# Moving the weights of the first sub-block of each group to another place in a 256-byte line

## The chip, the cores and the metric

The kernel runs on one NeuronCore of a Trainium2 chip. The metric is the device time of one execution in microseconds (us); lower is better. The kernel before takes 1067.77 us, the median of three runs (1066.1, 1067.77 and 1069.37 us).

## The reference

One layer of a decoder trunk in float32. The input x is 256 tokens by 2048 channels; sixteen learned tokens are put in front of it, so that 272 tokens pass through. With h the stream of tokens:

```
u = rms_norm(h, g1)
u = u @ w_in + b_in                    # 2048 -> 4096, split into a and g
u = a * sigmoid(g)
u = causal depthwise convolution of width 31 + b_dw
u = silu(layer_norm(u))
u = u @ w_out + b_out                  # 2048 -> 2048
h = h + rms_norm(u, g2)
u = rms_norm(h, g3)
u = (silu(u @ w_gate) * (u @ w_up)) @ w_down     # 2048 -> 5632 -> 2048
h = h + rms_norm(u, g4)                # the sixteen tokens are dropped at the end
```

Nearly all the arithmetic is in the four products with weights: "in" (w_in), "out" (w_out), "gu" (gate and up together) and "down".

## The kernel before

**Weights.** All weights come from HBM as one flat stream that the host laid out in the order of use. It is cut into 360 sub-blocks of 128 partitions by 1024 float32 (fewer where a block of the contraction ends). `plan()` (line 42) lists them: for each of the four products, for each group of output tiles, for each run of `kb` contraction tiles. A sub-block holds `kb` contraction tiles times `n` output tiles of 128 by 128. `load` (line 138) issues its DMA from SyncE into a ring of four raw tiles. `prep` (line 149) splits it: ScalarE rounds it to fp32r into the tile `hi` (line 158), then VectorE, or GpSimd for some, writes the rest `raw - hi` into the tile `lo` (line 160). Both tiles have rings of four buffers.

**Places.** A `hi` or `lo` buffer has 1024 + 64 elements for each partition (4352 bytes, 17 lines of 256 bytes), and the weights may begin at any of its first 64 elements. `PLACES` (line 61) gives the two starts in elements: "out" and "gu" have `hi` at 16 and `lo` at 0, which is 64 and 0 bytes; "in" has 0 and 128 bytes; "down" has 0 and 0. The activations that stream against them lie in the tile `moving`, whose rows are 2304 bytes long, nine lines of 256.

**Products.** In "out" and "gu" the weights are the stationary operand. The activations are split into a high and a low part in the same way, 256 columns each, side by side. Each 128 by 128 tile of weights takes two matmuls (a pair below): `hi` against 512 columns, high and low parts together (line 230), and `lo` against the 256 columns of the high part (line 231). Every matmul has its own weight load, because the weights change each time. "in" takes three matmuls of 272 columns for each tile (lines 221 to 223). The last group of "out" takes three matmuls of 256 columns (line 226). In "down" the activations are stationary and the weights stream, 512 columns at a time (lines 778 to 780).

**Groups.** "out" has six groups, of 4, 4, 4, 2, 1 and 1 output tiles; "gu" has 22 groups, each of two gate tiles and two up tiles. Sixteen contraction tiles make a full sum. A group of "gu" is 64 pairs in eight sub-blocks of eight pairs. The full groups of "out" are the same; the groups with 2, 1 and 1 tiles have 4, 2 and 2 sub-blocks, each with eight weight tiles. The first group of "out" and the first group of "gu" run while their activations are still being made (layer norm, and residual with RMS norm), so their matmuls wait for them here and there.

**Order.** The order on TensorE, ScalarE, VectorE and GpSimd is that of the program text. `ahead` keeps up to three sub-blocks prepared in front of the one in use. Work that empties the accumulators of a group is put into `pending` and done in stages at the ends of the next sub-blocks. One such stage in the second group of "gu" is `factor` (line 684): it holds an fp32 matmul (line 686) with a sum of squares, between the pairs of that group.

Of the kernel before, what the change touches and what calls it, by code (L numbers as in the profile page):

```python
# [41 lines left out]
def plan():  # L42
    out = []
    for name, groups, n_k in (
        ("in", IN_GROUPS, NK),
        ("out", OUT_GROUPS, NK),
        ("gu", FFN_GROUPS, NK),
        ("down", DOWN_GROUPS, NF),
    ):
        for g, tiles in enumerate(groups):  # L50
            n = len(tiles) * (2 if name == "gu" else 1)
            for k, kb in sub_blocks(n, n_k):
                out.append((name, g, n, k, kb))
    return out


PLAN = plan()
FIRST = {name: [p[0] for p in PLAN].index(name) for name in ("in", "out", "gu", "down")}

LINE = 64  # L60
PLACES = {"in": (0, 32), "out": (16, 0), "gu": (16, 0), "down": (0, 0)}
MOVE = 2 * L + 32


def places(name, g):
    return PLACES[name]


# [19 lines left out]
def conformer_swiglu_kernel(ctx: ExitStack, tc: tile.TileContext, xT, wflat, vec, w_dw, gain, out):  # L88
# [17 lines left out]
    def moving(cols, nm):  # L106

        t = xs.tile([P, NK, MOVE], F32R, tag="moving", name=nm)
        return t[:, :, :cols]
# [28 lines left out]
    def load(i):  # L138
        if i >= len(PLAN) or i in raws:
            return  # L140
        _, _, n, _, kb = PLAN[i]
        sz = n * kb * P
        raw = wp.tile([P, SB], F32, tag="raw", name="raw", bufs=RAW)
        nc.sync.dma_start(
            out=raw[:, :sz], in_=wflat[offs[i] : offs[i] + P * sz].rearrange("(p f) -> p f", p=P)
        )
        raws[i] = raw

    def prep(i):
        name, g, n, _, kb = PLAN[i]  # L150
        sz = n * kb * P
        for j in range(i, i + RAW):
            load(j)
        raw = raws.pop(i)
        hi_at, lo_at = places(name, g)
        hi = wp.tile([P, SB + LINE], F32R, tag="hi", name="hi")[:, hi_at : hi_at + SB]
        lo = wp.tile([P, SB + LINE], F32R, tag="lo", name="lo")[:, lo_at : lo_at + SB]
        nc.scalar.copy(out=hi[:, :sz], in_=raw[:, :sz])  # L158
        eng = nc.gpsimd if i < FIRST["out"] + 10 or 0 <= i - FIRST["gu"] < 10 else nc.vector
        eng.tensor_tensor(  # L160
            out=lo[:, :sz], in0=raw[:, :sz], in1=hi[:, :sz].bitcast(F32), op=ALU.subtract
        )
        ready[i] = (hi, lo)

    def ahead(i, n):

        while n and state["next"] <= min(i + LOOK, len(PLAN) - 1) and state["next"] < state["cap"]:
            prep(state["next"])
            state["next"] += 1
            n -= 1  # L170
# [571 lines left out]

    free = xs.tile([P, NK * MOVE], F32, tag="moving", name="free")
    tr = free[:, : NK * SEQ].rearrange("p (c t) -> p c t", c=NK)
# [178 lines left out]
```

## Time and profile before

| | |
|---|---|
| median of 3 runs | 1067.77 us |
| the profiled execution's own time | 1068.15 us |
| its span, first to last instruction | 1066.4 us |
| TensorE matmuls busy | 1052.4 us, 99% of the span |
| TensorE weight loads busy | 935.5 us, 88% |
| VectorE, ScalarE, GpSimd busy | 692.8, 584.1, 321.3 us |
| granted TensorE clock, mean | 0.998 |
| HBM read | 192.35 MB, 182 GB/s over the span |

A group of the profile is a source line on one engine, with the tiles that it writes and reads, the number of instructions, and their busy time. Matmuls are pipelined: the recorded length of one (0.28 us for 256 columns) overlaps the next. The number that tells the pace is the distance from one start to the next, which is the busy time of a gapless stretch divided by the number of pairs in it.

### The profile page before, as it was taken

Reading aid. Unit: us, or ns where it says so; the run is one execution under the profiler, and the core shown is the slowest. Engines: PE = TensorE matmul, PEld = TensorE weight load, DVE = VectorE, ACT = ScalarE, POOL = GpSimd, SP = SyncE. Lnnn points to the kernel's source line nnn. Section 1 sums busy time; section 2 is a strip of 40 time slices with the busy share of each in tenths; the row PEclk is TensorE's granted clock in tenths of the full one; section 3 lists DMA queues with packets and bytes.
Section 4 is the critical chain, followed back from the end, with each engine's and each line's share of the span. In section 5 each row is a group of like instructions: output and inputs, shape, how many; then the busy total and the mean of one; then the engine's idle time right before and its main releaser. Section 6 shows DMA issues by size and latency. Waiting matters only on the chain.

```text
span 1066.4 us, 16373 instructions
## 1 busy us (share of the span) xinstructions
PE 1052.4 (99%) x6142; PEld 935.5 (88%) x6142; DVE 692.8 (65%) x1193; ACT 584.1 (55%) x918; POOL 321.3 (30%) x191
## 2 busy tenths in 40 slices
PE   9999999999999999999999999999999999999996
PEld 8999999988898888888888888888888888888885
DVE  5699999987437966555665556655666635454544
ACT  6877877767567654444454445444444434343432
POOL 4889999955245112111111111111111000000000
PEclk9999999999999999999999999999999999999999
DMA  7555566526654666666666666666666797666662
GB/s 252 175 171 172 178 177 173 166 65 212 186 178 129 217 186 191 186 190 188 188 186 190 192 186 191 184 193 184 193 181 195 206 265 223 197 195 192 190 195 97
DMA packets 71840, 197.62 MB, mean 185 GB/s; under 512 B 22992, under 2 KB 24528, under 8 KB 71632
## 3 DMA queue, kind: packets, MB, share of 16 engines
q1 hardware_dynamic: 61728, 192.90, 60.7%
q10 hardware_dynamic: 10032, 3.67, 1.5%
q8 instruction: 48, 0.79, 0.3%
q14 instruction: 32, 0.26, 0.1%
HBM read 192.35 MB, written 2.10 MB: 182 GB/s over the span
## 4 chain that ended last, share of the span: by engine, by line
PE 96%; DVE 1%; DMA 1%; ACT 1%; issue 0%; SPq 0%; POOL 0%; DVEq 0%; ACTq 0%; POOLq 0%
PE bank L230 36%; PE bank L231 18%; PE bank L780 7%; PE bank L779 7%; PE bank L778 7%; PE bank L222 6%; PE bank L223 6%; PE bank L221 6%; DMA raw<-wflat 1%; PE bank L419 1%; PE bank L226 1%; ACT hi L158 0%; SPq L112 0%; POOL lo L160 0%; DVE free L835 0%
## 5 line engine op out<-in xcount | busy, mean ns | idle before, releaser
L158 ACT CAST hi<-raw 128x1024 fp32r<-128x1024 f32 x360 | 377.4, 1049 | 421.8 <-PE bank L230 189.3
L160 DVE TENSOR_TENSOR lo<-raw,hi 128x1024 fp32r<-128x1024 f32 x276 | 341.0, 1236 | 319.4 <-ACT hi L158 317.8
L230 PE MATMUL bank<-h_mv,hi 128*128 128x512 f32 x1408 | 492.2, 394 | 1.2 <-DVE h_mv L650 1.2
L231 PE MATMUL bank<-h_mv,lo 128*128 128x256 f32 x1408 | 395.1, 281 | 0.0
L230 PEld LDWEIGHTS bank<-h_mv,hi 128*128 128x128 f32 x1408 | 264.5, 188 | 60.6 <-issue 1.3
L231 PEld LDWEIGHTS bank<-h_mv,lo 128*128 128x128 f32 x1408 | 267.1, 190 | 0.0
L160 POOL TENSOR_TENSOR lo<-raw,hi 128x1024 fp32r<-128x1024 f32 x84 | 201.3, 2407 | 49.3 <-ACT hi L158 47.3
L720 POOL TENSOR_TENSOR hid<-sw_s,hid 128x256 fp32r<-128x256 f32 x44 | 64.8, 1474 | 416.2 <-ACT hid L719 416.2
L221 PE MATMUL bank<-x_mv,hi 128*128 128x272 f32 x512 | 147.6, 288 | 0.9 <-ACT x_mv L315 0.5
L222 PE MATMUL bank<-x_mv,hi 128*128 128x272 f32 x512 | 147.9, 289 | 0.4
L223 PE MATMUL bank<-x_mv,lo 128*128 128x272 f32 x512 | 147.7, 289 | 0.0
L778 PE MATMUL bank<-hi,hid 128*128 128x512 f32 x352 | 137.0, 389 | 0.0
L780 PE MATMUL bank<-hi,hid 128*128 128x512 f32 x352 | 136.9, 389 | 0.0
L779 PE MATMUL bank<-lo,hid 128*128 128x512 f32 x352 | 136.9, 389 | 0.0
L395 DVE SCALAR_TENSOR_TENSOR bank<-u,taps,bank 128x256 f32<-128x256 f32 x293 | 130.4, 489 | 1.7 <-ACT bank L388 1.7
L221 PEld LDWEIGHTS bank<-x_mv,hi 128*128 128x128 f32 x512 | 96.4, 188 | 2.1 <-ACT sig L354 1.0
L222 PEld LDWEIGHTS bank<-x_mv,hi 128*128 128x128 f32 x512 | 96.2, 188 | 1.1 <-DVE x_mv L316 1.1
L223 PEld LDWEIGHTS bank<-x_mv,lo 128*128 128x128 f32 x512 | 96.2, 188 | 0.0
L230 PE MATMUL bank<-s_mv,hi 128*128 128x512 f32 x240 | 84.8, 397 | 0.9 <-DVE s_mv L579 0.9
L778 PEld LDWEIGHTS bank<-hi,hid 128*128 128x128 f32 x352 | 66.1, 188 | 13.8
L779 PEld LDWEIGHTS bank<-lo,hid 128*128 128x128 f32 x352 | 66.1, 188 | 13.8
L780 PEld LDWEIGHTS bank<-hi,hid 128*128 128x128 f32 x352 | 66.1, 188 | 13.6
(139 smaller groups left out, 826.6 us busy)
## 6 DMA issues: line engine op xcount, KB each, us to landing
raw<-wflat SPq DMA_DIRECT2D x360, 512.0 KB, 3.6
x_sb<-xT SPq DMA_DIRECT2D x3, 544.0 KB, 4.9
x_sb<-free SPq DMA_DIRECT2D x16, 64.0 KB, 4.7
x_sb<-free ACTq DMA_DIRECT2D x16, 64.0 KB, 5.1
free<-gain ACTq DMA_DIRECT2D x1, 1024.0 KB, 8.5
y<-free ACTq DMA_DIRECT2D x8, 128.0 KB, 2.4
y<-free ACTq DMA_DIRECT2D x2, 256.0 KB, 2.4
y<-free SPq DMA_DIRECT2D x2, 256.0 KB, 2.8
```

Of the source, the lines that this page charges most:

```text
L158: nc.scalar.copy(out=hi[:, :sz], in_=raw[:, :sz])
L160: eng.tensor_tensor(out=lo[:, :sz], in0=raw[:, :sz], in1=hi[:, :sz].bitcast(F32), op=ALU.subtract)
L221: nc.tensor.matmul(banks[t][:, :L], lhsT=hi[:, s], rhs=xh[:, kk, :], start=kk == 0, stop=False)
L222: nc.tensor.matmul(banks[t][:, :L], lhsT=hi[:, s], rhs=xl[:, kk, :], start=False, stop=False)
L223: nc.tensor.matmul(banks[t][:, :L], lhsT=lo[:, s], rhs=xh[:, kk, :], start=False, stop=kk == n_k - 1)
L230: nc.tensor.matmul(banks[t], lhsT=hi[:, s], rhs=moving[:, kk, :], start=kk == 0, stop=False)
L231: nc.tensor.matmul(banks[t][:, :SEQ], lhsT=lo[:, s], rhs=moving[:, kk, :SEQ], start=False, stop=kk == n_k - 1)
L395: nc.vector.scalar_tensor_tensor(out=t if j == nd - 1 else o, in0=u[:, j : j + SEQ], scalar=taps[:, c, j : j + 1], in1=o, op0=ALU.mult, op ...
L720: nc.gpsimd.tensor_tensor(out=hl, in0=ts[2], in1=hh.bitcast(F32), op=ALU.subtract)
L778: nc.tensor.matmul(bs[h], lhsT=xh, rhs=hi[:, s], start=f == 0, stop=False)
L779: nc.tensor.matmul(bs[h], lhsT=xh, rhs=lo[:, s], start=False, stop=False)
L780: nc.tensor.matmul(bs[h], lhsT=xl, rhs=hi[:, s], start=False, stop=f == NF - 1)
```

## The change

The first sub-block of each group of "gu", and of each group of "out" but the first, has its `hi` part at element 0 and its `lo` part at element 48 (0 and 192 bytes of a line of 256). All other sub-blocks keep their places. No instruction is added, removed or reordered; the tiles keep their sizes. 27 of the 360 sub-blocks are touched: 22 in "gu" and 5 in "out".

```diff
 LINE = 64
 PLACES = {"in": (0, 32), "out": (16, 0), "gu": (16, 0), "down": (0, 0)}
+OTHER = (0, 48)
 MOVE = 2 * L + 32
 
-def places(name, g):
+def places(name, g, k0, kb):
+    if k0 == 0 and (name == "gu" or name == "out" and g):
+        return OTHER
     return PLACES[name]
...
     def prep(i):
-        name, g, n, _, kb = PLAN[i]
+        name, g, n, k0, kb = PLAN[i]
...
-        hi_at, lo_at = places(name, g)
+        hi_at, lo_at = places(name, g, k0, kb)
```

## Rows read from the trace of the kernel before

**Rows 1.** The page: span, busy time by engine, granted clock by slice, chain's engines

```profile
span 1066.4 us, 16373 instructions
...
PE 1052.4 (99%) x6142; PEld 935.5 (88%) x6142; DVE 692.8 (65%) x1193; ACT 584.1 (55%) x918; POOL 321.3 (30%) x191
...
PEclk9999999999999999999999999999999999999999
...
PE 96%; DVE 1%; DMA 1%; ACT 1%; issue 0%; SPq 0%; POOL 0%; DVEq 0%; ACTq 0%; POOLq 0%
```

**Rows 2.** Groups by line, TensorE, 400 to 800 us (gu): count, busy us, mean ns

```profile
L230 PE MATMUL bank<-h_mv,hi 128*128 128x512 f32 x1144 | 400.4, 394 | 0.0
L231 PE MATMUL bank<-h_mv,lo 128*128 128x256 f32 x1143 | 321.2, 281 | 0.0
```

**Rows 3.** The same, 335 to 360 us (gu, groups 0 and 1)

```profile
L230 PE MATMUL bank<-h_mv,hi 128*128 128x512 f32 x75 | 25.5, 389 | 0.0
L231 PE MATMUL bank<-h_mv,lo 128*128 128x256 f32 x74 | 20.4, 276 | 0.0
```

**Rows 4.** Timeline of TensorE, 361 to 363.3 us: start, length, line

```profile
360.64 0.39 PE L230 MATMUL bank<-h_mv,hi 128*128 128x512 f32 x1
...
360.98 0.39 PE L230 MATMUL bank<-h_mv,hi 128*128 128x512 f32 x1
361.21 0.28 PE L231 MATMUL bank<-h_mv,lo 128*128 128x256 f32 x1
361.42 0.67 PE L686 MATMUL bank<-acc,ones 128*128 128x256 f32 x2
361.74 0.58 PE L230 MATMUL bank<-h_mv,hi 128*128 128x512 f32 x1
...
362.27 0.40 PE L230 MATMUL bank<-h_mv,hi 128*128 128x512 f32 x1
...
362.97 0.40 PE L230 MATMUL bank<-h_mv,hi 128*128 128x512 f32 x1
```

**Rows 5.** Timeline of TensorE, 229 to 233 us (start of out)

```profile
229.20 0.50 PE L230 MATMUL bank<-s_mv,hi 128*128 128x512 f32 x1 [0.94 <-DVE s_mv L579]
229.54 0.28 PE L231 MATMUL bank<-s_mv,lo 128*128 128x256 f32 x1
```

**Rows 6.** Timeline of TensorE, 245 to 249.8 us (out, group 0)

```profile
245.30 0.40 PE L230 MATMUL bank<-s_mv,hi 128*128 128x512 f32 x1
...
246.72 0.47 PE L230 MATMUL bank<-s_mv,hi 128*128 128x512 f32 x1
```

**Rows 7.** Timeline of TensorE, 322 to 331.5 us (start of gu)

```profile
327.26 0.45 PE L230 MATMUL bank<-h_mv,hi 128*128 128x512 f32 x1
327.55 0.28 PE L231 MATMUL bank<-h_mv,lo 128*128 128x256 f32 x1
327.66 0.39 PE L230 MATMUL bank<-h_mv,hi 128*128 128x512 f32 x1
...
331.06 0.39 PE L230 MATMUL bank<-h_mv,hi 128*128 128x512 f32 x1
```

**Rows 8.** Groups by line, TensorE, 253 to 313 us (out, groups 1 to 4)

```profile
L230 PE MATMUL bank<-s_mv,hi 128*128 128x512 f32 x173 | 60.6, 395 | 0.0
```

**Rows 9.** Busy time by stretch: PE, PEld, DVE, ACT, POOL, clock, DMA share, GB/s

```profile
100.00:200.00 100.00, 100.00 (x798) 100.00 (x797) 97.11 (x259) 78.16 (x149) 96.16 (x52) 1.00 0.60 174
...
500.00:600.00 100.00, 100.00 (x573) 87.80 (x573) 61.31 (x82) 47.69 (x73) 11.79 (x8) 1.00 0.63 189
...
830.00:1030.00 200.00, 200.00 (x884) 165.62 (x883) 99.25 (x92) 82.17 (x88) 0.00 (x0) 1.00 0.74 210
```

**Rows 10.** Waits, 400 to 800 us: who for whom, total us, times, longest

```profile
DVE lo L160 <- ACT hi L158: 157.7, 127, 1.6
ACT hi L158 <- PE bank L230: 147.1, 90, 1.8
```

## The prediction

> **What bounds the kernel now.** I read the page first. [...] The change alters no count of matmuls or columns, only where in a line of 256 bytes some weights lie; what it can change is the distance from one matmul's start to the next.
>
> I therefore read that distance next, from gapless stretches: busy time over count. From 400 to 800 us, in "gu", a pair (one `hi` matmul of 512 columns, one `lo` matmul of 256) takes 400.4 / 1144 = 350.0 ns [rows 2]. From 335 to 360 us the same pair takes 25.5 / 75 = 340.0 ns [rows 3]. [...]
>
> The timeline shows where the one becomes the other. Up to 360.98 us `hi` matmuls start 340 ns apart; then the fp32 matmul of `factor` comes between, and from 362.27 us on they start 350 ns apart [rows 4]. Nothing brings the pace back: rows 2 still have 350.0 over 1144 pairs. "out" shows the same number, 60.6 / 173 = 350.3 ns [rows 8]. The pace is thus something into which the stream falls after a disturbance, and which it keeps. The timeline of the two starts of "out" and "gu", where matmuls wait for activations, says more: I count 16 restarts after such a wait (the first at 229.20 us [rows 5], the one before the last at 327.26 us [rows 7], the last that of rows 4). After 7 of them the pairs follow at 340 ns, after 8 at 350, after one at (246.72 - 245.30) / 4 = 355 [rows 6]. The restart of rows 7 shows the good case: from 327.66 to 331.06 us there are ten pairs, 340 each.
>
> What differs between the paces must be how the weight loads of the next matmul fall against the columns that stream for the present one; both are read from the same memory at the same time. That is my inference. The rows show three paces, not their cause.
>
> **The change, part by part.** *Instructions.* None is added or removed. ScalarE's and VectorE's writes of the 27 moved sub-blocks go to other bytes of the same buffers. I take that at nothing, and it is covered: in "gu" ScalarE stands waiting for TensorE to free a buffer for 147.1 us of 400 [rows 10], so the weights lie ready ahead of use. Without that cover a sub-block would have to be late by more than such a wait (up to 1.8 us) before TensorE saw it.
>
> *The first sub-blocks themselves.* 22 x 8 = 176 pairs in "gu", 4 x 8 = 32 in "out" (groups 1 to 4), and 24 single matmuls in the last group of "out". No row shows a pair with weights at 0 and 192 bytes. Bounds: 340 from below [rows 3], 355 from above [rows 6]. [...] Between them and the 350 of now I take 350, that is no gain. The bounds, over the 192 pairs that now run at 350 (20 groups of "gu", 4 of "out"), are 192 x -10 = -1.9 us and 192 x +5 = +1.0 us.
>
> *The two seams of each such sub-block.* Weights at 64 and 0 are followed by weights at 0 and 192, and eight pairs later the other way round. Both parts move by 64 bytes in the same direction (64 to 0, and 0 to 192 of the line before), so the distance between `hi` and `lo` in a line stays, but both move against the streaming columns. A seam is a disturbance of just the kind to which the rows react, without the wait. I price it from zero to one short restart: in rows 7 `hi` to the next `hi` is 327.66 - 327.26 = 0.40 us, 0.06 over a pair. At 2 x 27 seams that is at most 3.2 us; I take zero, because no operand is late there.
>
> *The pairs after the seam.* This is the term that decides. If the stream leaves the first sub-block in the 340 pace and keeps it, as it does over 335 to 360 us, then 20 groups of "gu" (2 to 21) gain 56 pairs each, 1120 x 10 ns = 11.2 us, and "out" gains 56 + 56 + 24 + 8 = 144 pairs x 10 = 1.4 us. Group 1 of "gu" falls back to 350 at `factor` as now, since its first sub-block comes before it; group 0 and the front of group 1 are at 340 already. The last group of "out" and "down" I leave as they are: 48 short matmuls cannot move 0.3 us, and "down" has no moved weights. Sum: 0 + 0 - 11.2 - 1.4 = -12.6 us.
>
> *What would be late next.* At 340 ns a sub-block of "gu" lasts 2.72 us instead of 2.80. From 500 to 600 us VectorE is busy 61%, ScalarE 48%, DMA 0.63 at 189 GB/s [rows 9]; 3% more leaves all three far from full. "down" reads 210 GB/s. So the gain is not taken back by another engine.
>
> The profiled execution took 1068.15 us, 0.4 above the median of the runs, so the sum is made against it: 1068.15 - 12.6 = 1055.5 us.
>
> [...]
>
> **The rivals.**
>
> *Nothing changes (1068).* The loss depends on when a weight load starts, not on where it reads; or the moved sub-blocks find 350 too and the stream comes back to 350 at each second seam. For it: 350 has held across every boundary of groups and of buffers [rows 2], so the stream is stable in it. Against it: the same stream left its pace at 16 disturbances. Time: 1068.15 with the bounds of the first sub-blocks, 1066.2 to 1069.2. [...]
>
> *Half of it (1062).* A seam taken at 340 may throw the stream out again, so that groups alternate: half of 12.6 us, 1061.9.
>
> *Slower (1077).* The seam puts the stream into the 355 pace, which also exists [rows 6], and holds it there: 20 x 64 pairs of "gu" and 176 of "out" at +5 make 7.3 us; the some 100 pairs of groups 0 and 1 of "gu" that are now at 340 lose 15 ns each, 1.5 us; together 1077.0. It decides from the first seam of "out" on, at the second group. For it: both losses at a seam are unknown. Against it: one restart of 16 went there. A milder form: the pace stays at 350, and the seams cost 0.06 us each: 3.2 us, 1071.4.
>
> **How the numbers follow.** Restarts alone would give 340 in 7 cases of 16, 350 in 8, 355 in 1. A seam is repeated 27 times with the same addresses; if it leads from 350 to 340 anywhere and not back, the stream stays good, which raises the good case above its share. I give the forecast 0.43, half of it 0.10, nothing 0.25, slower 0.22 (0.12 for 355, 0.10 for the seams' price). A measurement of this kernel can tell about 0.3%, 3.2 us, from no change. Faster by more than that: 0.43 + 0.10 = 0.53. Within it: 0.25, and 0.02 of the seams' price. Slower: 0.20. The forecast's own range is 1053 (first sub-blocks at 340 too: -14.5) to 1059.7 (both unknowns at their dear ends, +1.0 and +3.2). The range for 8 in 10 goes from 1052 to 1074; it leaves out most of the 355 case above and a pace below 340 beneath.
>
> **What would show it.** Right: from 400 to 800 us some 1176 pairs instead of 1144, with the mean recorded lengths 389 and 276 of rows 3 in place of 394 and 281; "down" begins some 12 to 13 us earlier, and its own pace is unchanged. In the timeline the change of pace stands at the start of a group. The first sub-block step is right if its eight pairs take 8 x 350 = 2.8 us; the seams, if no `hi` follows a `hi` there by more than 0.36 us. Wrong: pairs at 350 outside the first sub-blocks, or at 355; or TensorE with idle time in front of line 230 that names a weight tile, which would mean that the cover of rows 10 did not hold.

## The result and the profile after

The changed kernel takes 1054.48 us (median of 1054.46, 1054.48 and 1054.89) against 1067.77; the ratio is 0.9868 with a 95% interval of 0.9844 to 0.9891. It is faster by 13.3 us; 1055.5 was forecast. Its profiled execution took 1054.46 us, against 1068.15 for the one before.

The page of the changed kernel (span, busy times by engine, the chain's shares by engine) answers to [rows 1]; the source lines have moved by four, so 230 and 231 are now 234 and 235.

```profile
span 1052.7 us, 16373 instructions
...
PE 1038.2 (99%) x6142; PEld 925.1 (88%) x6142; DVE 691.9 (66%) x1193; ACT 584.5 (56%) x918; POOL 322.2 (31%) x191
...
PE 96%; DVE 1%; DMA 1%; ACT 1%; issue 0%; SPq 0%; POOL 0%; DVEq 0%; ACTq 0%; POOLq 0%
```

TensorE still bounds the kernel and is still busy all the time; its busy time is 14.2 us shorter, with the same 6142 matmuls. VectorE, ScalarE and GpSimd have what they had.

Groups by line on TensorE in the changed kernel, 400 to 780 us ("gu", to be held against [rows 2]), then 253 to 313 us ("out", against [rows 8]):

```profile
L234 PE MATMUL bank<-h_mv,hi 128*128 128x512 f32 x1116 | 380.4, 390 | 0.0
L235 PE MATMUL bank<-h_mv,lo 128*128 128x256 f32 x1115 | 307.9, 276 | 0.0
...
L234 PE MATMUL bank<-s_mv,hi 128*128 128x512 f32 x174 | 59.4, 390 | 0.0
```

380.4 / 1116 = 340.9 ns a pair where it was 350.0, and 59.4 / 174 = 341.4 where it was 350.3. The mean is not 340 because of the moved sub-blocks. The timeline of TensorE around the start of group 8 of "gu" (start, length, line) shows them:

```profile
498.63 0.39 PE L234 MATMUL bank<-h_mv,hi 128*128 128x512 f32 x1
...
498.97 0.39 PE L234 MATMUL bank<-h_mv,hi 128*128 128x512 f32 x1
...
499.31 0.40 PE L234 MATMUL bank<-h_mv,hi 128*128 128x512 f32 x1
...
502.08 0.39 PE L234 MATMUL bank<-h_mv,hi 128*128 128x512 f32 x1
...
502.42 0.39 PE L234 MATMUL bank<-h_mv,hi 128*128 128x512 f32 x1
```

Before the group, 340 ns from `hi` to `hi`; then eight pairs in 502.08 - 499.31 = 2.77 us, 346 each (346.7 as the mean over the groups from 3 on); behind them 340 at once. Neither seam costs anything when the moved sub-block is entered at 340: the first pair on either side already has the pace of its side.

Where the 13.7 us of span came from is read off the first matmul of each stage. After ("out", "gu", "down"):

```profile
229.05 0.50 PE L234 MATMUL bank<-s_mv,hi 128*128 128x512 f32 x1 [0.94 <-DVE s_mv L583]
...
324.10 0.47 PE L234 MATMUL bank<-h_mv,hi 128*128 128x512 f32 x1 [1.18 <-DVE h_mv L654]
...
804.70 0.40 PE L782 MATMUL bank<-hi,hid 128*128 128x512 f32 x1
```

and the last two of these places in the kernel before (its "out" begins at 229.20 us, [rows 5]):

```profile
325.79 0.47 PE L230 MATMUL bank<-h_mv,hi 128*128 128x512 f32 x1 [1.18 <-DVE h_mv L650]
...
818.32 0.40 PE L778 MATMUL bank<-hi,hid 128*128 128x512 f32 x1
```

"gu" begins 1.7 us earlier, "down" 13.6 us earlier, and the end 13.7. Of the 1.7 us, 0.15 lie before "out", where nothing was changed. So "out" gave about 1.5, "gu" 11.9, and "down" with the tail (247.98 us against 248.05) next to nothing.

### The profile page after: what moved, and what is told of

Read it like the earlier page. It is cut to its first block, busy times and chain, and to the rows that moved or that the text cites. A ratio compares the mean times of both kernels' runs of the same rounds, so it can differ in the third digit from the quotient of the medians.

```text
span 1052.7 us, 16373 instructions
## 1 busy us (share of the span) xinstructions
PE 1038.2 (99%) x6142; PEld 925.1 (88%) x6142; DVE 691.9 (66%) x1193; ACT 584.5 (56%) x918; POOL 322.2 (31%) x191
## 4 chain that ended last, share of the span: by engine, by line
PE 96%; DVE 1%; DMA 1%; ACT 1%; issue 0%; SPq 0%; POOL 0%; DVEq 0%; ACTq 0%; POOLq 0%
PE bank L234 36%; PE bank L235 18%; PE bank L782 8%; PE bank L783 8%; PE bank L784 8%; PE bank L226 6%; PE bank L225 6%; PE bank L227 6%; DMA raw<-wflat 1%; PE bank L423 1%; PE bank L230 1%; ACT hi L162 0%; SPq L116 0%; POOL lo L164 0%; DVE free L839 0%
## 5 line engine op out<-in xcount | busy, mean ns | idle before, releaser
L164 DVE TENSOR_TENSOR lo<-raw,hi 128x1024 fp32r<-128x1024 f32 x276 | 340.9, 1235 | 306.8 <-ACT hi L162 304.8
L234 PE MATMUL bank<-h_mv,hi 128*128 128x512 f32 x1408 | 480.4, 390 | 1.2 <-DVE h_mv L654 1.2
L235 PE MATMUL bank<-h_mv,lo 128*128 128x256 f32 x1408 | 388.9, 276 | 0.0
L235 PEld LDWEIGHTS bank<-h_mv,lo 128*128 128x128 f32 x1408 | 264.3, 188 | 0.0
L782 PEld LDWEIGHTS bank<-hi,hid 128*128 128x128 f32 x352 | 66.1, 188 | 13.7
L783 PEld LDWEIGHTS bank<-lo,hid 128*128 128x128 f32 x352 | 66.1, 188 | 13.6
```

Source lines behind the costliest of these rows:

```text
L164: eng.tensor_tensor(out=lo[:, :sz], in0=raw[:, :sz], in1=hi[:, :sz].bitcast(F32), op=ALU.subtract)
L234: nc.tensor.matmul(banks[t], lhsT=hi[:, s], rhs=moving[:, kk, :], start=kk == 0, stop=False)
L235: nc.tensor.matmul(banks[t][:, :SEQ], lhsT=lo[:, s], rhs=moving[:, kk, :SEQ], start=False, stop=kk == n_k - 1)
L782: nc.tensor.matmul(bs[h], lhsT=xh, rhs=hi[:, s], start=f == 0, stop=False)
L783: nc.tensor.matmul(bs[h], lhsT=xh, rhs=lo[:, s], start=False, stop=False)
```

## The experiments

The theory under test, A: in each product TensorE's stream has a few steady paces, which depend on how the weights lie in a line of 256 bytes against the columns that stream; a disturbance may throw the stream from one to another, and it then stays. The moved sub-block gains by what it leaves behind, not by its own place. The edits below are made to the changed kernel, and the source lines move with them. The added disturbance and the four maps of places were executed once each, so of them the paces count and not the times.

### One moved sub-block

```diff
-    if k0 == 0 and (name == "gu" or name == "out" and g):
+    if k0 == 0 and name == "gu" and g == 2:
         return OTHER
```

> Only the first sub-block of group 2 of gu lies at 0 and 192 bytes; out and all else as before. Theory A (the pace is a state: a seam brings the stream to 340 ns a pair, and it stays there by itself): 350 until group 2, its first sub-block near 347, then 340 through group 21; gain 1272 pairs x 10 ns and 8 x 3, 12.7 us, 1055 us. Rival B (each group needs its own moved sub-block; the pace falls back to 350 at the next group's start): group 2 alone gains, 56 x 10 ns, 1067 us. Rival C (the gain is in the moved sub-blocks' own place): 1067.7 us.

Measured: 1055.98 us (1054.11 to 1057.21), ratio to before 0.9885 [0.9869, 0.9902]. Groups by line of this kernel, 325 to 360 us, then 375 to 780 us:

```profile
L234 PE MATMUL bank<-h_mv,hi 128*128 128x512 f32 x101 | 35.4, 395 | 0.0
...
L234 PE MATMUL bank<-h_mv,hi 128*128 128x512 f32 x1192 | 405.3, 389 | 0.0
```

and its "out", 255 to 300 us, where no sub-block is moved:

```profile
L234 PE MATMUL bank<-s_mv,hi 128*128 128x512 f32 x134 | 45.6, 389 | 0.0
```

350 ns before group 2, and 405.3 / 1192 = 340.0 for all that follows it: one sub-block of eight pairs changes the pace of the 1272 others of groups 2 to 21 by 10 ns each. B and C are out. A lucky restart is out as the cause too: the 37 executions of the kernel before that are on record took 1066.1 to 1073.5 us, and all four of this one took 1057.21 or less. The profiled one, the fastest of the four, was lucky in "out" besides: there it ran at 340 without a moved sub-block, which is worth up to 1.8 us (176 pairs at 10 ns). In the nine traces with no moved sub-block in "out", its groups 1 to 4 ran at 350 four times, at 340 three times and at 353.3 twice.

Entered from 350, the moved sub-block's own pairs took 352.2 ns on average and those of the next sub-block 341.1, which is 26 ns more than eight pairs at 350 and eight at 340. It is not the seams alone: the first six pairs follow at 355, 351, 347, 356, 351 and 346 ns, 351 on average, a second pace of the moved place, which the next experiment shows as well.

### All of "gu" in the moved place, and the columns moved instead of the weights

```diff
-    if k0 == 0 and (name == "gu" or name == "out" and g):
+    if name == "gu":
         return OTHER
```

> All of gu lies at 0 and 192 bytes, out as before. Theory A (in the moved place the stream has a steady pace of its own, 346.6 ns a pair as in the first sub-blocks of the changed kernel): 346.6 ns from the end of group 0 on, 1068 - 1280 x 3.4 ns + 100 x 6.6 ns, about 1064 us. Rival C (the place is the better one and the stream gets to 340 in it): 340 ns, 1055 us or less.

```diff
-    if k0 == 0 and (name == "gu" or name == "out" and g):
-        return OTHER
...
-    def moving(cols, nm):
+    def moving(cols, nm, at=0):
...
-        return t[:, :, :cols]
+        return t[:, :, at : at + cols]
...
-    h_mv = moving(2 * SEQ, "h_mv")
+    h_mv = moving(2 * SEQ, "h_mv", 16)     # the slice of the tile begins at element 16
```

> The weights lie as before; the activations of gu begin 64 bytes further on in their rows, so that the weights stand to them as in the moved sub-blocks (64 bytes back). Theory A (what counts is the place of the weights in a line as against that of the streaming columns): the pace of the moved sub-blocks, 346.6 ns a pair, about 1064 us, and the same paces as the kernel with all of gu at 0 and 192 bytes. Rival D (the place of the weights in the line counts by itself): a pace of the kernel before, 340 or 350 ns, 1055 or 1068 us.

The first took 1069.68 us (ratio 1.0001 [0.9986, 1.0016]), the second 1068.44 us (0.9993 [0.9979, 1.0006]). Groups by line of the kernel with all of "gu" moved, 330 to 358 us and 400 to 800 us:

```profile
L234 PE MATMUL bank<-h_mv,hi 128*128 128x512 f32 x82 | 28.5, 396 | 0.0
...
L234 PE MATMUL bank<-h_mv,hi 128*128 128x512 f32 x1140 | 400.3, 396 | 0.0
```

and of the kernel with the columns moved, 330 to 358 us and 400 to 790 us:

```profile
L232 PE MATMUL bank<-h_mv,hi 128*128 128x512 f32 x81 | 28.5, 396 | 0.0
...
L232 PE MATMUL bank<-h_mv,hi 128*128 128x512 f32 x1126 | 390.4, 396 | 0.0
```

(A window of 28 us holds parts of pairs at its edges; from start to start these paces are 346.7 in the first kernel and 351.1 in the second.) "Out", which neither kernel changes, ran at 353.3 in both traces. In "gu" each kernel changes pace once, at the fp32 matmul of `factor`, in opposite directions: the first from 346.7 to 400.3 / 1140 = 351.1, the second from 351.1 to 390.4 / 1126 = 346.7. So the two have the same pair of paces, 346.7 and 351.1, and neither 340 nor 350. Moving the columns forward does what moving the weights back does: for this one step of 64 bytes, what counts is their place against each other. D is out. So is another rival, the writes: ScalarE and VectorE write the weights of the second kernel to the places of the kernel before, and its paces are those of the first. C is out too: the stream does not get to 340 in the place that the change introduces, and at its 351.1 a whole stage takes as long as in the old one at 350. The times that A gave, 1064 us, were missed, since I had counted on one pace in that place and it has at least two. The eight executions of the second kernel lie at 1064.3 and 1065.0 and, six of them, from 1068.3 to 1069.5 us; the profiled one is of the first kind.

### A disturbance without moved weights

```diff
         banks = [bank() for _ in range(4)]
+        if g >= 2:
+            wd = 6 * (g - 1)
+            nc.tensor.matmul(banks[0][:, :wd], lhsT=ones, rhs=ones[:, :wd], start=True, stop=True)
         matmuls("gu", g, banks, h_mv, NK, before=residual if g == 0 else None)
```

(No sub-block is moved here.)

> The weights lie as before everywhere. From group 2 of gu on, one fp32 matmul of 6 x (g - 1) columns (6 to 120) stands ahead of each group's first pair; its result is overwritten by that pair. Theory A (the pace is a state, and any disturbance can change it): some groups run at 340 ns, some at 350, perhaps some at 355, each from its matmul to the next, about half at 340. Rival E (only moved weights bring the stream from 350 to 340): all twenty groups stay at 350. By A the time is about 1067 us (6 us gained, 4 to 6 lost in the added matmuls), by E 1072 us.

Measured: 1067.96 us. The timeline at the start of group 7, where the added matmul has 36 columns, and the groups by line of 440 to 457 us (group 5), 483 to 499 us (group 7) and 505 to 521 us (group 8):

```profile
479.69 0.39 PE L232 MATMUL bank<-h_mv,hi 128*128 128x512 f32 x1
479.92 0.28 PE L233 MATMUL bank<-h_mv,lo 128*128 128x256 f32 x1
480.04 0.31 PE L730 MATMUL bank<-ones 128*128 128x36 f32 x2
480.18 0.48 PE L232 MATMUL bank<-h_mv,hi 128*128 128x512 f32 x1
```

```profile
L232 PE MATMUL bank<-h_mv,hi 128*128 128x512 f32 x51 | 17.4, 389 | 0.0
...
L232 PE MATMUL bank<-h_mv,hi 128*128 128x512 f32 x47 | 16.5, 395 | 0.0
...
L232 PE MATMUL bank<-h_mv,hi 128*128 128x512 f32 x48 | 16.4, 389 | 0.0
```

Groups 2 to 6, 8 and 20 run at 340.0, the other thirteen at 350.0, each from its own added matmul to the next. With the weights of the kernel before, group 8 came back from 350 to 340 and group 20 as well. So E is out: moved weights are one way to throw the stream over, and 340 belongs to the old place. But ten of the twelve added matmuls that met a stream at 350 left it there.

### Which places have which paces

In two kernels groups 2 to 17 of "gu" have sixteen pairs of places, in rising and in falling order.

```diff
-    if k0 == 0 and (name == "gu" or name == "out" and g):
-        return OTHER
+    if name == "gu" and 2 <= g < 18:       # and with 17 - g for g - 2 in the other kernel
+        return 16 * ((g - 2) // 4), 16 * ((g - 2) % 4)
```

> Each of groups 2 to 17 of gu has a pair of places of its own in all its sub-blocks: group 2 + 4a + b has hi at 64a and lo at 64b bytes; the other groups are as before. Theory A (the pace depends on where both parts lie against the streaming columns): different steady paces by group, 340 or 350 in group 6 (64 and 0), 346.6 or 351.1 in group 5 (0 and 192), and paces of other sizes, 333 to 360 ns, elsewhere. Rival F (only the distance from hi to lo in a line counts): the four groups with one distance (for 64 and 0: groups 5, 6, 11 and 16) show the same paces.

> The same sixteen pairs of places in the opposite order, so that each is entered from another state. Theory A (a place allows one or a few paces, and which one is taken depends on how it is entered): where a place allows one pace, it shows the same in both runs; where it allows two, the runs may differ. A rival in which the pace depends on the place alone has the same pace for each pair of places in both runs.

They took 1065.82 and 1069.46 us. The steady pace of each pair of places, worked out from the starts of the matmuls in ns a pair (rising order / falling order):

```
hi at      lo at 0          64              128             192 bytes
  0     353 / 346.7    346.7 / 346.7   346.7 / 346.7    350 / 350
 64     340 / 350      353.3 / 353.3   350   / 350      353.3 / 353.3
128     352 / 352      346.7 / 353.3   351.2 / 351.2    346.7 / 346.7
192     340 / 350      346.7 / 346.7   346.7 / 346.7    353.5 / 348.9
```

Group 6 of the first kernel (462 to 481 us) and group 13 of the second (618 to 639 us) have the same old place, 64 and 0:

```profile
L234 PE MATMUL bank<-h_mv,hi 128*128 128x512 f32 x57 | 19.4, 389 | 0.0
...
L234 PE MATMUL bank<-h_mv,hi 128*128 128x512 f32 x61 | 21.4, 394 | 0.0
```

Five of the sixteen differ between the two orders, so that their pace depends on how they were entered, the old place among them; 0 and 192 shows 350 in both, a third pace beside the 346.7 and 351.1 of the experiments above. F is out: the four with the distance of 64 and 0 (at 0/192, 64/0, 128/64, 192/128) have 350, 340 or 350, 346.7 or 353.3, and 346.7. No place showed a pace under 340, and only two showed 340; each was entered twice, so that others may have it too. In the falling order groups 18 to 21, back in the old place, stay at a third pace of it. Groups by line, 775 to 796 us of that kernel:

```profile
L234 PE MATMUL bank<-h_mv,hi 128*128 128x512 f32 x61 | 21.6, 396 | 0.0
```

From start to start that is 353.3 ns, and it is what I had read as 355 from four pairs with a restart at their end [rows 6].

### Which moved sub-blocks bring 340

```diff
-    if k0 == 0 and (name == "gu" or name == "out" and g):
-        return OTHER
+    if k0 == 0 and name == "gu" and 2 <= g < 18:
+        return 16 * ((g - 2) // 4), 16 * ((g - 2) % 4)
```

> Weights at 64 and 0 bytes as before, and only the first sub-block of groups 2 to 17 of gu lies elsewhere, at one of the sixteen pairs of places (group 2 + 4a + b: hi at 64a, lo at 64b bytes). Theory A (any seam may set the pace, each to a fixed one): after each first sub-block a steady 340, 350 or 355 ns that depends on the place and on the pace before. Rival G (the place 0 and 192 alone brings 340): 350 up to group 5, 340 from there on, unless another seam takes it away.

Measured: 1059.98 us. Fifteen moved sub-blocks (group 6 has the old place), each entered once. Groups by line, 482 to 501 us (group 7, behind a sub-block at 64/64) and 529 to 546 us (group 9, behind one at 64/192):

```profile
L234 PE MATMUL bank<-h_mv,hi 128*128 128x512 f32 x55 | 19.3, 395 | 0.0
...
L234 PE MATMUL bank<-h_mv,hi 128*128 128x512 f32 x51 | 17.4, 389 | 0.0
```

From 350 or 353 the places 0/192, 64/192, 128/64, 128/192 and 192/128 led to 340; 0/0, 0/64, 0/128 and 64/128 did not. From 340 the places 64/64, 128/0, 128/128 and 192/64 led away to 350 or 353; 192/0 and 192/192 kept it. G is out. The pace that follows depends on the place, and a moved sub-block can as well take 340 away. The place that the change uses did both things that it needs in every trace here: it led from 350 to 340 and from 340 to 340, and from 353.3 to 340 as well ("out" of the next run of the changed kernel, "out" and "gu" of the last kernel below).

### The fewest moved sub-blocks

```diff
-    if k0 == 0 and (name == "gu" or name == "out" and g):
+    if k0 == 0 and (name, g) in (("out", 1), ("gu", 2)):
         return OTHER
```

> Only two sub-blocks lie at 0 and 192 bytes: the first of group 1 of out and the first of group 2 of gu. Theory A (each seam sets the pace once, and it stays): as the changed kernel without 25 of its 27 moved sub-blocks, each of which costs 8 x 6.6 ns; 1054.5 - 25 x 0.053 = 1053.2 us if groups 0 and 1 of gu are at 340, up to 0.8 us more if at 350. Rival B (the pace falls back unless it is set anew in each group): 1066 us.

Measured: 1053.25, 1053.28, 1054.27, 1054.35 and 1059.29 us; ratio to before 0.9862 [0.9845, 0.9878]. In the trace both stages run at 340 behind their one moved sub-block, as A has it; B is out again. Groups 0 and 1 of "gu" were at 350 in it, which A priced at up to 0.8 us. No measurement here tells it from the changed kernel. The profiled execution is the one of 1059.29 us, and its loss lies in "down", where nothing was changed. Busy time by stretch (PE, PEld, DVE, ACT, POOL, clock, DMA share, GB/s) of this execution:

```profile
860.00:867.00 7.00, 7.00 (x33) 5.79 (x32) 2.89 (x3) 3.59 (x4) 0.00 (x0) 1.00 1.09 254
867.00:873.00 6.00, 3.81 (x15) 2.27 (x13) 1.47 (x2) 1.82 (x2) 0.00 (x0) 1.00 0.79 323
873.00:877.00 4.00, 3.64 (x9) 2.92 (x10) 4.00 (x6) 3.32 (x7) 0.00 (x0) 0.57 0.67 190
```

TensorE waits there, 1.7 us at the longest, for weights that came late (ScalarE's longest wait for `raw` was 4.7 us), while the transfers of the transposed residual were in the DMA queues. Behind these waits, from 873 to 877 us, the granted clock is 0.57 on average; in the changed kernel it is 1.00 in the same stretch. The other kernels make the same transfers, and the changed one was busy without a gap there, 10.0 of the 10 us from 867 to 877; why the weights came late in this execution is open.

### The change once more

> The changed kernel once more, as the standard for the run beside it and for the spread of its times: about 1054.5 us, with 340 ns a pair after each moved sub-block in every execution (theory A), so a spread under 1 us; if the pace that it finds is a matter of luck, single executions at 1060 us or more.

The kernel is the changed one as it is. Measured: 1054.73 us (1054.37 to 1055.29), beside 1069.52 for the kernel before on the same chip; 0.9857 [0.9837, 0.9876]. Its trace shows what repeating the moved sub-block is good for. The fp32 matmul of `factor` threw this execution from 340 to 350, and group 2 brought it back. Groups by line, 358.5 to 368.5 us (behind `factor`), then 391 to 412 us:

```profile
L234 PE MATMUL bank<-h_mv,hi 128*128 128x512 f32 x29 | 10.4, 400 | 0.0
L235 PE MATMUL bank<-h_mv,lo 128*128 128x256 f32 x28 | 7.8, 280 | 0.0
L690 PE MATMUL bank<-acc,ones 128*128 128x256 f32 x2 | 0.7, 416 | 0.0
```

```profile
L234 PE MATMUL bank<-h_mv,hi 128*128 128x512 f32 x63 | 21.5, 390 | 0.0
```

From start to start the pairs right behind `factor` are at 350 and those from group 2's second sub-block on at 340, moved sub-blocks apart. No execution is near 1060 us.

### The places of "in" and "down"

```diff
-    if k0 == 0 and (name == "gu" or name == "out" and g):
-        return OTHER
+    if name == "in":
+        return 16 * (g // 4), 16 * (g % 4)
+    if name == "down" and g * 22 + k0 // 2 < 80:
+        j = (g * 22 + k0 // 2) // 5
+        return 16 * (j // 4), 16 * (j % 4)
```

> out and gu as in the kernel before. Group g of in has hi at 64 (g // 4) and lo at 64 (g % 4) bytes; in down the same sixteen pairs of places come one after another, five sub-blocks (60 matmuls) each. Theory A (what is lost beside the columns depends on how weight loads and streaming columns lie to each other in a line of 256 bytes): several paces in both stages, in 'in' about 120 to 130 ns a matmul against 125.7 now, in 'down', where the weights are what streams, about 220 to 235 ns against 226.7. Rival H (the places matter only where the two matmuls of a pair differ in length, as in out and gu): 125.7 and 226.7 throughout.

Measured: 1069.57 us. Both stages have paces too, so H is out. Each pair of places was entered once. From start to start "in" runs between 123.3 ns a matmul (192 and 0 bytes) and 126.7 (0/64, 0/192, 128/128, 128/192), "down" between 226.7 (0 and 0, as it is) and 234.4 (192 and 0). That points to a version with another place in "in":

```diff
-PLACES = {"in": (0, 32), "out": (16, 0), "gu": (16, 0), "down": (0, 0)}
+PLACES = {"in": (48, 0), "out": (16, 0), "gu": (16, 0), "down": (0, 0)}
```

(the moved sub-blocks of the change are kept)

> The changed kernel, and besides the weights of in at 192 and 0 bytes, the pair with the least distance in the map of in (123.3 ns a matmul against 125.7). Theory A (the pace of a place holds through the whole stage): 1536 matmuls x 2.4 ns = 3.7 us less than the changed kernel where no other wait sets the end, 1050.8 us, and at least half of it. Rival I (in is held by VectorE, 97% busy there, and what TensorE gains is lost again in waits): 1054.5 us.

Measured: 1051.29 us (1051.17 to 1051.32), ratio to before 0.9824 [0.9808, 0.984]. It beats the changed kernel, run beside it on the same chip, by 3.4 us. Busy time by stretch of it, 100 to 200 us, against the first of [rows 9]:

```profile
100.00:200.00 100.00, 100.00 (x813) 100.00 (x812) 98.86 (x262) 79.74 (x151) 97.57 (x52) 1.00 0.60 179
```

813 matmuls in 100 us instead of 798, with VectorE at 99%. Rival I is out for this step: 3.4 of the 3.7 us came. With VectorE at 99% little seems left for a next one, which no run tried.

## Why the prediction was right

*The bound and the unit.* Right: TensorE was busy 99% of the span before [rows 1] and after, the span fell by what TensorE's pairs lost, no wait took its place, and "down" kept its pace, 884 matmuls in 200 us. VectorE went from 61% to 64% in 500 to 600 us.

*The pairs after the seam.* This term carried the forecast, and its mechanism is what the runs show: 20 groups x 56 pairs x 10 ns, and 1.4 us in "out". The single moved sub-block shows it alone. That the seam would bring 340, and no other pace, was not worked out; it was the chance of 0.43. The map of moved sub-blocks shows how much of this was luck: of nine places entered from 350 or 353 five brought 340, and of six entered at 340 four lost it. 0 and 192 brings and keeps it, which nothing in the prediction's rows told.

*The first sub-blocks.* I took 350, an estimate between the bounds that no row and no run of the changed kernel shows: its moved sub-blocks have 346.7 (groups from 3 on), so 192 x 3.3 = 0.6 us more was gained. This is about half of the difference from the forecast. The 16 pairs in groups 0 and 1 of "gu" that stood at 340 already lost 0.1 us, a term that the sum left out.

*The seams.* Taken at zero. Between 340 and the moved place they cost nothing. Entered from 350, as in the first moved sub-block of "out", the moved sub-block and the next took together 0.05 us more than at 346.7 and 340.

*Group 1 behind `factor`.* I had it fall back to 350 as before. In the first trace of the changed kernel it stayed at 340, some 0.3 us better; in the second it fell back. That was luck: eleven traces here have the old place in group 1 behind `factor`, and in the ten others the pairs there are at 350 or 353.

*Sum.* -11.2 - 1.4 - 0.6 - 0.3 + 0.1 = -13.4. The 13.7 us of span have 0.15 before "out" and 0.07 in "down" and the tail besides, where nothing was changed; the rest is rounding. In the prediction's own range, 1068.15 - 14.5 is 1053.7, not 1053.

*The rivals.* "Slower" rested on a real pace, 353.3 rather than 355, but the moved sub-block does not lead there. "Half of it" is out, since the seam holds 340 when it is entered at 340. "Nothing changes" fell with the first run. What stood against it, that the stream left its pace at 16 disturbances, was read too high: 16 restarts were counted, and in the trace before only eight of them change the pace. Sixteen places of the weights, with the same instructions, gave from 340 to 353.5 ns a pair, against its first form, in which the loss (here the 10 ns from 340 to 350) does not depend on where a weight load reads.

*What stays open.* That the pace depends on the place and on history is shown (340 to 353.5 ns a pair over sixteen places, five of which differ between the two orders), and for one step of 64 bytes that the place against the columns is what counts (346.7 and 351.1 in both kernels). What makes a pair longer in one place than in another is not shown by any run; the prediction has an inference on it, which stays one. Nor is it explained why one place leads from 350 to 340 and another does not.

## What to carry to other kernels

Where TensorE is busy without a gap, divide busy time by matmuls in several stretches of the same code: two paces with the same instructions, here 340 and 350 ns, point to a cause outside them. Map the places of the operands inside a line by giving each group of a loop another one in a single run, and enter each place from more than one state, because one pace seen once is not the pace of the place: here five of sixteen places showed two. Where a stream keeps the pace into which it fell, try to set it again by a short stretch at another place: here eight pairs at 0 and 192 bytes took it from 350 to 340 ns, while other places took it from 340 to 350 or 353. Repeat the stretch behind what disturbs the stream, as the fp32 matmul of `factor` did in the second trace of the changed kernel, from 340 to 350.

## What the runs showed of the hardware that was not expected

The pace held: 1192 pairs at 340.0 ns behind one moved sub-block, and 1144 at 350.0 without it, the latter with VectorE busy 61%, ScalarE 48%, GpSimd 12% and the DMAs 0.63 in 500 to 600 us [rows 9]. Places that differ by multiples of 64 bytes, together with what came before, changed a pair by up to 4% in "gu" (340 to 353.5), and a matmul by 3% in "down" (226.7 to 234.4). The place that was the best in "in", 192 and 0 bytes (123.3 ns), was the worst in "down" (234.4 ns). The old place of "gu" alone has three paces, 340, 350 and 353.3.
